# Moving a finished block's store and its subtractions behind the next statistics stores in GpSimd's queue

## The chip, the cores and the metric

The kernel runs on one core of one Trainium2 chip. The time is the device time of one execution in microseconds (us). Before the change it is 1297.03 us, the median of three runs that lie between 1296.88 and 1305.32 us.

Engines have short names in the profile: PE is TensorE (matrix products; PEld is its weight load), DVE is VectorE, ACT is ScalarE, POOL is GpSimd, and SP is SyncE, which here only issues transfers. A name with a q (SPq) is an engine's sequencer, which issues and waits. Each engine works through its own queue in order: an instruction that waits holds everything behind it on that engine.

## The reference

One layer with two branches over 1024 tokens of width 1024, in float32: a Mamba-2 scan and a causal attention with a forgetting term. Both are gated, projected, merged and projected again:

```python
h = _rmsnorm(x, pre_g)
proj = jnp.einsum('bld,de->ble', h, w_in)   # z_ssm, xbc, dt, q, k, v, f, z_att, g_ssm, g_att
# branch A: y_ssm = group-normed SSD scan, times silu(z_ssm)
# branch B, 16 heads of 64, blocks of 128 queries:
s = q @ k.T * scale + fcum[t] - fcum[s]      # causal
o = softmax(s) @ v
y_att = o * silu(z_att)
p_ssm = y_ssm @ w_branch_ssm
p_att = y_att @ w_branch_att
merged = sigmoid(g_ssm) * p_ssm + sigmoid(g_att) * p_att
out = x + _rmsnorm(merged @ w_out, post_g)
```

## The kernel before

**The projections.** All large products (the input projection, the two branch projections, the output projection) are made of 128x512 tiles with a seven-product scheme for 2x2 blocks (Winograd's form of Strassen's). For it, each right-hand operand is cut into four blocks `b11, b12, b21, b22`, and differences `t1 = b12 - b11`, `t2 = b22 - t1`, `t3 = t2 - b11`, `t4 = t2 - b21` are formed. Each operand is split into a high and a low part (`x0h`, `x0l` for b11, `x1` for b21, `x2` for -b22, `x3` for t1, `x4` for -t2, `x5` for t3, `x6` for t4) and multiplied three times. A `Stream` object doles these products out in halves, as work that fills TensorE while a latency-bound stage runs.

**The attention.** It runs over eight head pairs `hp` (two heads, 128 channels, 1024 tokens), from about 690 to 1150 us of the span. For seven pairs there are five visits each (`JOINED`, line 1384); the last pair has six (`SINGLE`). A visit makes scores `s` (TensorE), adds the forgetting term and takes a row minimum (VectorE, line 1558, tiles `ex`, `nm`), takes the exponential (ScalarE, line 1563), transposes the result (TensorE, `pt`), copies it out of PSUM (`p`, lines 1600 and 1602) and multiplies it with `v` into `av`. Between its parts, fixed numbers of stream halves are placed. A pair's output comes in three groups n = 0, 1, 2, which end with its visits g = 1, 3 and 4. Groups 0 and 1 make up the second half of the tokens (h = 1), group 2 is the first half (h = 0). For each group:

- `settle` and `scale` (lines 1436 to 1455) make the softmax denominators from small tiles: `nr`, `dd`, `sm`, `ns`, of 128x4 and 128x8 elements;
- `send` (line 1457) transposes `ns` (`tp`), copies the 8x128 result to `st` (ScalarE, line 1463) and stores it in DRAM with two transfers from GpSimd's queue (line 1465): a row of statistics;
- `take` (line 1467) loads it back, spread over 64 partitions each (`rb`, line 1471, SyncE's queue);
- `free` (line 1482) multiplies `av` by the gate `zr` into `o`, which frees the PSUM bank (line 1490);
- `out` (line 1492) multiplies `o` by `rb`: lines 1502 and 1503 for n = 0 and 1, line 1496 for n = 2. After n = 1 and n = 2 a half of the pair's output stands in the tile `zr`, which has two buffers, and `outputs` (line 1629) is called.

**A finished block.** For all pairs but the last, `outputs` stores the half to `ya_dram` (line 1633, GpSimd's queue) and makes the differences that the branch projection needs later, on GpSimd: for pairs 0 to 3 `t1` from h = 0 alone (line 1639, on a tile `y` that is loaded from `ya_dram`), for pairs 4 to 6 `t2` and `t3` after h = 1 (lines 1645 and 1646) and `t4` after h = 0 (line 1659), on a tile `x` of one buffer, which holds `t1`. Results are stored later as chores of the stream (line 196). GpSimd also makes the like differences of the other branch in this stage (line 214), sums of weights (line 364) and transfers to `ms_dram` (line 1104).

**What sets the order.** The main loop (line 1722) goes through the visits m. In each it makes scores, then calls `out` for the group that ended two visits ago, then `weighted`, then `free` and `send` for the group that ended one visit ago. So `out(1)` of a pair and `send(2)` of the same pair fall into one iteration, in that order; `out(2)` falls into the next one, where nothing is sent; `send(0)` of the next pair comes an iteration later. Operations in `pin(...)` keep their program order on their engine. The others (SyncE's loads among them, lines 266, 1477, 1679) are placed by a scheduler, by its own estimate of when they can run. `attended` records which halves are stored; a block of `ya_dram` is loaded as an operand only after that (lines 297 to 315).

## Time and profile before

| What | us |
| --- | --- |
| median of three runs | 1297.03 |
| the profiled execution, whole | 1297.4 |
| its span, first to last instruction | 1295.6 |
| PE busy | 1251.2 (97%) |
| DVE busy | 1018.6 (79%) |
| ACT busy | 796.9 (62%) |
| POOL busy | 288.6 (22%) |

The granted TensorE clock is 0.996 in the mean. All times in the text are us from the first instruction of this execution. In a row of the timeline stand the start, the time taken, the engine, the line, the operation and its tiles; in brackets stands how long the engine had been idle before it and what ended that. In rows of waits stand the engine that waited, what it waited for, the sum, the number of times and the longest.

### The profile page before, as it was taken

The page shows a single profiled execution, that of the slowest core. Times are in us where ns is not written, and L with a number is a line of the kernel's source. Part 1 is how long each engine was busy: PE and PEld are TensorE (multiplying, and loading weights), DVE is VectorE, ACT ScalarE, POOL GpSimd, SP SyncE. Part 2 cuts the span into 40 slices and gives each one's busy share as a digit, 9 for nine tenths or more (in the row PEclk, how much of TensorE's full clock was granted, in tenths as well). Part 3 has the DMA queues.
Part 4 walks back from the last instruction along what each step waited for, and adds up shares of the span by engine and source line. Part 5 has one row for each costly group of instructions (what it writes and reads, how often), then busy time and mean ns, then how long its engine had stood idle before and what let it go on. Part 6 is the DMA issues. An engine that isn't in the chain of part 4 may idle for free.

```text
span 1295.6 us, 21107 instructions
## 1 busy us (share of the span) xinstructions
PE 1251.2 (97%) x7066; PEld 987.7 (76%) x7066; DVE 1018.6 (79%) x1979; ACT 796.9 (62%) x1728; POOL 288.6 (22%) x307
## 2 busy tenths in 40 slices
PE   6999999999999999899999999999998999999998
PEld 4787888788887888688777777777777777678886
DVE  6998888798789878788677767676677877886976
ACT  8745666476556756566556566666667656753754
POOL 0000330024102320133001222222120313246052
PEclk9999999999999999999999999999999999999999
DMA  7332443654463544455474765666587657765932
GB/s 280 100 108 82 146 149 120 199 139 147 130 205 114 159 149 164 121 150 151 160 246 149 243 193 167 229 212 205 194 275 249 214 191 245 245 209 194 369 110 102
DMA packets 154669, 233.60 MB, mean 180 GB/s; under 512 B 17216, under 2 KB 62656, under 8 KB 154560
## 3 DMA queue, kind: packets, MB, share of 16 engines
q1 hardware_dynamic: 142016, 205.53, 49.5%
q0 software_dynamic: 6400, 16.10, 3.3%
q10 hardware_dynamic: 6144, 10.62, 2.2%
q8 instruction: 56, 0.92, 0.3%
q14 instruction: 53, 0.43, 0.1%
HBM read 162.99 MB, written 72.34 MB: 182 GB/s over the span
## 4 chain that ended last, share of the span: by engine, by line
PE 66%; DVE 10%; DMA 9%; issue 7%; ACT 6%; SPq 1%; POOL 1%; ACTq 0%; DVEq 0%; POOLq 0%
PE pb L130 28%; PE pc L130 16%; PE pd L130 5%; PE pt L133 4%; PE s L130 4%; PE av L130 4%; PE yps L130 2%; DVE wop L357 2%; DMA raw<-in_wu 1%; PE tr L133 1%; ACT ex L1563 1%; PE st L130 1%; ACT wop L355 1%; DMA rb<-st_dram 1%; DVE sum L364 1%
## 5 line engine op out<-in xcount | busy, mean ns | idle before, releaser
L357 DVE TENSOR_TENSOR wop<-sum,wop 128x512 fp32r<-128x512 f32 x174 | 137.8, 793 | 59.7 <-ACT wop L355 56.4
L355 ACT ACTIVATE wop<-sum 128x512 fp32r<-128x512 f32 x174 | 108.9, 627 | 99.5 <-DVE sum L364 48.3
L1563 ACT ACTIVATE ex<-ex,nm 128x512 f32<-128x512 f32 (+1 forms) x192 | 116.1, 606 | 58.5 <-DVE nm L1558 55.5
L412 ACT ACTIVATE s<-pb 128x512 f32<-128x512 f32 x141 | 83.7, 594 | 99.0 <-PE pb L130 82.3
L357 DVE TENSOR_TENSOR wop<-raw,wop 128x512 fp32r<-128x512 f32 x149 | 108.3, 729 | 42.6 <-ACT wop L355 42.3
L130 PE MATMUL pc<-x3h,wop 128*128 128x512 f32 x384 | 131.2, 398 | 3.4 <-ACT wop L355 2.0
L130 PE MATMUL pb<-x0h,wop 128*128 128x512 f32 x384 | 133.0, 402 | 0.7 <-ACT x0h L1253 0.6
L130 PE MATMUL pc<-x2h,wop 128*128 128x512 f32 x384 | 131.9, 400 | 0.0
L130 PE MATMUL pb<-x6h,wop 128*128 128x512 f32 x376 | 128.7, 398 | 1.2 <-ACT s L412 1.2
L130 PE MATMUL pb<-x5h,wop 128*128 128x512 f32 x376 | 127.9, 397 | 1.4 <-ACT s L412 1.3
L130 PE MATMUL pb<-x4h,wop 128*128 128x512 f32 x376 | 127.8, 397 | 0.2 <-DVE wop L357 0.2
L355 ACT ACTIVATE wop<-raw 128x512 fp32r<-128x512 f32 x151 | 94.1, 625 | 19.1 <-PE pc L130 9.2
L1558 DVE CUSTOM_DVE_ANT_0 ex<-s,fb 128x512 f32<-128x512 f32 (+1 forms) x192 | 96.4, 552 | 10.8 <-PE s L130 10.7
L130 PE MATMUL pd<-x1h,wop 128*128 128x512 f32 x264 | 89.1, 396 | 0.0
L130 PEld LDWEIGHTS pc<-x3h,wop 128*128 128x128 f32 x384 | 72.1, 188 | 21.5 <-issue 3.4
L130 PEld LDWEIGHTS pb<-x0h,wop 128*128 128x128 f32 x384 | 73.1, 190 | 17.4 <-ACT x0h L1253 1.3
L130 PEld LDWEIGHTS pc<-x2h,wop 128*128 128x128 f32 x384 | 72.1, 188 | 16.8 <-issue 1.5
L130 PEld LDWEIGHTS pb<-x5h,wop 128*128 128x128 f32 x376 | 70.6, 188 | 17.9 <-ACT s L412 2.7
L130 PEld LDWEIGHTS pb<-x6h,wop 128*128 128x128 f32 x376 | 70.9, 189 | 16.9 <-ACT s L412 1.6
L130 PEld LDWEIGHTS pb<-x4h,wop 128*128 128x128 f32 x376 | 70.4, 188 | 16.4 <-DVE wop L357 1.0
L214 POOL TENSOR_TENSOR wd<-wd 128x256 f32<-128x256 f32 x32 | 31.8, 995 | 226.9 <-DMA wd<-in_wo 107.7
L130 PE MATMUL s<-k,q 64*128 64x512 f32 (+3 forms) x576 | 72.8, 367 | 5.9 <-ACT p L1602 3.3
(341 smaller groups left out, 3015.1 us busy)
## 6 DMA issues: line engine op xcount, KB each, us to landing
raw<-in_wu SPq DMA_DIRECT2D x128, 256.0 KB, 3.8
csb<-cs_dram SPq DMA_DIRECT2D x32, 256.0 KB, 5.4
fb<-f_dram SPq DMA_DIRECT2D x16, 512.0 KB, 6.1
rb<-st_dram SPq DMA_DIRECT2D x48, 128.0 KB, 3.5
wd<-in_wo SPq DMA_DIRECT2D x40, 128.0 KB, 3.2
xt<-in_x SPq DMA_DIRECT2D x8, 512.0 KB, 5.8
gs_dram<-th ACTq DMA_DIRECT2D x16, 256.0 KB, 3.4
qh_dram<-th SPq DMA_DIRECT2D x16, 256.0 KB, 4.2
```

Source lines behind the costliest of these rows:

```text
L130: return tc.keep_in_program_order(nc.tensor.matmul(*args, **kw))
L133: return tc.keep_in_program_order(nc.tensor.transpose(out_, in_, idn))
L214: pin(nc.gpsimd.tensor_tensor(t[out_], t[a_], t[b_], ALU.subtract))
L355: nc.scalar.activation(op[:, 0], src, AF.Copy, scale=sign)
L357: nc.vector.tensor_tensor(op[:, 1], src, op[:, 0], ALU.subtract)
L364: self.adds.tensor_tensor(t, x, y, ALU.add)
L412: nc.scalar.activation(s, ps, AF.Copy)
L1558: nc.vector.tensor_tensor_reduce(to, bank(u, e), fb[hp, h][:, e, 0 : w[u]], 1.0, 3.0e38, ALU.add, ALU.min, nm)
L1563: nc.scalar.activation(to, to, AF.Exp, scale=-1.0, bias=nm, accum_out=hd.at(hd.sm, i, h, e))
```

## The change

`outputs` no longer issues the store and the subtractions of pairs 0 to 6. It puts them on a list, `behind_rows`, and the main loop issues them right after the next `send`. The arithmetic is the same. For pairs 0 to 3 the load of `y` stays where it was. The last pair's subtractions are on VectorE, as before.

```diff
         def outputs(hp, h, zr):
+            if hp < NK - 1:
+                y = fetched("b12", hp) if hp < KH and h == 0 else state.get("y")
+                behind_rows.append(lambda: differences(hp, h, zr, y, state.get("t")))
+                return
             attended.add((hp, h))
-            if hp < NK - 1:
-                pin(nc.gpsimd.dma_start(ya_dram[hp, :, half(h)], zr))
-
-            eng = nc.vector if hp == NK - 1 else nc.gpsimd
+            j, x, y = hp - KH, state["t"], state["y"]
+            pin(nc.vector.tensor_tensor(x, zr, x, ALU.subtract))
+            pin(nc.vector.tensor_tensor(y, x, y, ALU.subtract))
+            ops_a.put(j, t2=x, t3=y, b22=zr)
+
+        behind_rows = []
+
+        def differences(hp, h, zr, y, x):
+
+            attended.add((hp, h))
+            pin(nc.gpsimd.dma_start(ya_dram[hp, :, half(h)], zr))
             if hp < KH:
                 if h == 0:
-                    y = fetched("b12", hp)
                     pin(nc.gpsimd.tensor_tensor(y, y, zr, ALU.subtract))
                     stream.chores += [None, lambda: ops_a.store("t1", hp, y)]
                 return
...
                 hd.free(which)
                 if m < NV:
                     hd.send(which)
+                    while behind_rows:
+                        behind_rows.pop(0)()
             stream.release()
```

GpSimd's queue about the end of pair 0 and the beginning of pair 1, before. The first row stores the half h = 1, the second group 2's statistics, the fifth and sixth handle h = 0, and the last stores the statistics of pair 1's group 0; line 214 belongs to the other branch.

```order
L1633 DMA ya_dram<-zr 128x512
L1465 DMA st_dram<-st 2x2x128 x2
L214 TENSOR_TENSOR x<-x,th 128x512
L196 DMA t_s<-x 128x512
L1633 DMA ya_dram<-zr 128x512
L1639 TENSOR_TENSOR y<-y,zr 128x512
L214 TENSOR_TENSOR x<-x,th 128x512
L1465 DMA st_dram<-st 2x2x128 x2
```

The same place of the same queue now (line 1633 has become 1646, line 1639 has become 1649):

```order
L1465 DMA st_dram<-st 2x2x128 x2
L1646 DMA ya_dram<-zr 128x512
L214 TENSOR_TENSOR x<-x,th 128x512
L196 DMA t_s<-x 128x512
L214 TENSOR_TENSOR x<-x,th 128x512
L1465 DMA st_dram<-st 2x2x128 x2
L1646 DMA ya_dram<-zr 128x512
L1649 TENSOR_TENSOR y<-y,zr 128x512
```

Group 2's statistics no longer stand behind the store of h = 1, and the store and the subtraction of h = 0 have moved behind the statistics of the next pair.

GpSimd's queue at the end of pair 4, before, where h = 1 has two subtractions and h = 0 one:

```order
L1633 DMA ya_dram<-zr 128x512
L1645 TENSOR_TENSOR x<-zr,x 128x512
L1646 TENSOR_TENSOR y<-x,y 128x512
L1465 DMA st_dram<-st 2x2x128 x2
L196 DMA t_a<-x 128x512
L196 DMA t_a<-y 128x512
L1633 DMA ya_dram<-zr 128x512
L1659 TENSOR_TENSOR x<-x,zr 128x512
L196 DMA t_a<-x 128x512
L1465 DMA st_dram<-st 2x2x128 x2
```

And now (1645 has become 1654, 1646 has become 1655, 1659 has become 1664):

```order
L1465 DMA st_dram<-st 2x2x128 x2
L1646 DMA ya_dram<-zr 128x512
L1654 TENSOR_TENSOR x<-zr,x 128x512
L1655 TENSOR_TENSOR y<-x,y 128x512
L196 DMA t_a<-x 128x512
L196 DMA t_a<-y 128x512
L1465 DMA st_dram<-st 2x2x128 x2
L1646 DMA ya_dram<-zr 128x512
L1664 TENSOR_TENSOR x<-x,zr 128x512
L196 DMA t_a<-x 128x512
```

Both statistics stores now stand ahead of the work on the block beside them.

ScalarE's queue early in the last pair, as a piece of the difference. `x1h<-x1l` splits a b21 block that was loaded from `ya_dram`; `ex` is the exponential of the scores:

```order
 L412 ACTIVATE s<-pb 128x512
 L355 ACTIVATE wop<-raw 128x512
-L281 ACTIVATE x1h<-x1l 128x512 x2
-L1563 ACTIVATE ex,sm<-ex,nm 128x512 x4
+L281 ACTIVATE x1h<-x1l 128x512
+L1563 ACTIVATE ex,sm<-ex,nm 128x512
+L281 ACTIVATE x1h<-x1l 128x512
+L1563 ACTIVATE ex,sm<-ex,nm 128x512 x3
 L278 ACTIVATE x4h<-x4l 128x512
 L281 ACTIVATE x1h<-x1l 128x512
```

The second split, which is of the block of pair 6, h = 0, now stands between the first exponential of the visit and the other three. In SyncE's queue, the load of that block has moved from ahead of group 0's two `rb` loads to behind them. TensorE's queue holds the same instructions in the same order as before.

## The prediction

> **What bounds the kernel now.** I read the busy table first. These are its first two lines: the span, and each engine's busy time.

> ```profile
> span 1295.6 us, 21107 instructions
> PE 1251.2 (97%) x7066; PEld 987.7 (76%) x7066; DVE 1018.6 (79%) x1979; ACT 796.9 (62%) x1728; POOL 288.6 (22%) x307
> ```

> TensorE is the bound, and it has 1295.6 - 1251.2 = 44.4 us of idle time in all. Its queue is unchanged, so the change can only fill or widen these gaps. Where they lie is told by the busy time per stage; this is the attention from 700 to 1140 us (stage, its length, busy PE, PEld, DVE, ACT, POOL, clock, DMA share, GB/s):

> ```profile
> 700.00:1140.00 440.00, 424.68 (x2891) 324.68 (x2889) 325.02 (x813) 286.79 (x710) 100.28 (x134) 1.00 0.66 219
> ```

> 440.0 - 424.7 = 15.3 us. This is the ceiling of any gain here: 1.2% of the time. It is further out of reach since the waits of TensorE from 690 to 1150 us name neither GpSimd nor a transfer:

> ```profile
> PE pt L133 <- ACT ex L1563: 3.4, 3, 1.9
> PE s L130 <- ACT p L1602: 3.3, 2, 2.8
> PE s L130 <- DVE p L1600: 2.5, 4, 1.0
> ...
> PE pc L130 <- DVE th L422: 0.5, 1, 0.5
> ```

> So I looked for what stands behind the gaps. The timeline about the largest of them (2.77 us) shows it, engine by engine: TensorE, VectorE, ScalarE, GpSimd, at the end of pair 0.

> ```profile
> 744.51 1.98 PE L130 MATMUL s<-k,q 64*128 64x512 f32 x12 [2.77 <-ACT p L1602]
> ...
> 737.14 0.69 DVE L1496 TENSOR_TENSOR zr<-o,rb 128x512 f32<-128x512 f32 x1 [1.41 <-DMA rb<-st_dram]
> ...
> 738.35 2.92 DVE L1436 TENSOR_TENSOR nr<-nm 128x4 f32<-128x4 f32 x1
> ...
> 741.58 0.21 ACT L1439 ACTIVATE dd<-dd 128x8 f32<-128x8 f32 x1 [5.00 <-DVE dd L1438]
> ...
> 738.14 0.58 POOL L1633 DMA_DIRECT2D ya_dram<-zr  x1 [7.75 <-DVE zr L1496]
> 738.73 1.29 POOL L1639 TENSOR_TENSOR y<-y,zr 128x512 f32<-128x512 f32 x1
> 739.97 1.28 POOL L214 TENSOR_TENSOR x<-x,th 128x512 f32<-128x512 f32 x1
> ```

> The chain reads: VectorE sits 1.41 us for the statistics `rb`; then `nr`, four elements a partition, takes 2.92 us and ends as GpSimd's two subtractions end (739.97 + 1.28 = 741.25); ScalarE, whose `dd` comes next in its queue, is idle 5.00 us; the copies `p` behind it are late; TensorE waits 2.77 us. All executions of that line on VectorE, with least, median and longest time in ns:

> ```profile
> L1436 DVE TENSOR_TENSOR nr<-nm x15: 154/156/2924, 703.8 to 1113.5; 128x4 f32<-128x4 f32 x15
> ```

> The median is 0.156 us, so `nr` was held for 2.77 us. Two things on this chain are touched by the change: the wait for `rb`, and the subtraction of h = 0.

> **The change part by part.**

> *Statistics ahead of the store of h = 1 (seven pairs).* How often line 1496 waits for `rb` is in VectorE's waits of the stage:

> ```profile
> DVE zr L1496 <- DMA rb<-st_dram: 8.3, 6, 2.4
> ```

> The longest is pair 6, again by engines: ScalarE, GpSimd, VectorE, TensorE.

> ```profile
> 1081.54 0.25 ACT L1463 ACTIVATE st<-tp 8x128 f32<-8x128 f32 x1
> ...
> 1081.81 0.57 POOL L1633 DMA_DIRECT2D ya_dram<-zr  x1 [3.26 <-DVE zr L1503]
> 1082.39 1.30 POOL L1645 TENSOR_TENSOR x<-zr,x 128x512 f32<-128x512 f32 x1
> 1083.78 1.62 POOL L1646 TENSOR_TENSOR y<-x,y 128x512 f32<-128x512 f32 x1
> 1085.35 1.17 POOL L1465 DMA_DIRECT2D st_dram<-st  x2
> ...
> 1093.53 0.69 DVE L1496 TENSOR_TENSOR zr<-o,rb 128x512 f32<-128x512 f32 x1 [2.39 <-DMA rb<-st_dram]
> ...
> 1100.14 0.55 PE L130 MATMUL s<-k,q 64*128 64x128 f32 x6 [1.00 <-DVE p L1600]
> ```

> `st` is ready at 1081.79, yet its store goes out at 1085.35. Ahead of the block's work it can go some 3.3 us sooner, more than the 2.39 us of the wait. For pairs 0 to 3 only the store's issue (0.57 us) and the wait for the block stand ahead of it, so there it gains less than in pairs 4 to 6; I take the 8.3 us as gone. It is VectorE's time, not TensorE's: what it is worth is the gap that follows.

> *Subtractions of h = 0 out of the denominator chain (seven).* They now run some 13 us later (738.7 becomes 752.2 below). Besides pair 0, pair 3 shows the hold (`sm` on VectorE, then TensorE):

> ```profile
> 904.46 2.82 DVE L1450 TENSOR_TENSOR sm<-sm,dd 128x8 f32<-128x8 f32 x1 [0.28 <-ACT dd L1439]
> ...
> 909.15 1.66 PE L130 MATMUL s<-k,q 64*128 64x512 f32 x11 [0.70 <-DVE p L1600]
> ```

> TensorE's gaps within some 7 us behind a line 1496 that waited are then 2.77 (pair 0), 0.70 (pair 3), 1.00 (pair 6) and the 0.5 for `th`, line 422 (pair 4): 4.97 us at most. Of this I count 4 us, since line 214 stays and will still hold something, and the gaps of 1.00 and 0.5 have a nearer cause of their own.

> *Where they go.* Behind the statistics of the next pair, here pair 1 (GpSimd, then VectorE):

> ```profile
> 750.49 1.15 POOL L1465 DMA_DIRECT2D st_dram<-st  x2 [9.24 <-ACT st L1463]
> ...
> 752.52 0.69 DVE L357 TENSOR_TENSOR wop<-raw,wop 128x512 fp32r<-128x512 f32 x1 [2.91 <-ACT wop L355]
> ```

> The subtraction would run from 750.49 + 1.15 + 0.58 = 752.2 to 753.5 and hold `wop` of line 357 for about 1 us. `wop` is prepared three steps of the stream ahead, and VectorE has been idle 2.91 us before it. Such holds exist now: 45 of these have a mean of 802 ns against 686 for the like `wop<-sum`,

> ```profile
> L357 DVE TENSOR_TENSOR wop<-raw,wop 128x512 fp32r<-128x512 f32 x45 | 36.1, 802 | 32.9 <-ACT wop L355 32.8
> L357 DVE TENSOR_TENSOR wop<-sum,wop 128x512 fp32r<-128x512 f32 x35 | 24.0, 686 | 10.7 <-ACT wop L355 8.0 <-PE s L130 2.7
> ```

> so 45 x 0.116 = 5.2 us are lost there already, while TensorE's waits above name no `wop`. I put this at 0; if the cover is gone, it is 7 x 1.29 = 9.0 us at the very most. The store of h = 0 moves with it: `zr` has two buffers, and its reload moves behind `rb` in SyncE's queue. I price that at 0, bounded by the next part.

> *The last pair.* This part costs. The block of pair 6, h = 0, is stored later, and its split has landed between two exponentials. Rows of GpSimd, SyncE, ScalarE, TensorE:

> ```profile
> 1104.29 1.17 POOL L1465 DMA_DIRECT2D st_dram<-st  x2 [3.39 <-ACT st L1463]
> ...
> 1104.11 1.33 SPq L266 DMA_DIRECT2D x1l<-ya_dram  x3
> 1108.76 1.09 SPq L1471 DMA_DIRECT2D rb<-st_dram  x2
> ...
> 1108.76 1.14 ACT L281 ACTIVATE x1h<-x1l 128x512 fp32r<-128x512 f32 x2
> 1110.64 0.73 ACT L1563 ACTIVATE ex<-ex,nm 128x512 f32<-128x512 f32 x1
> ...
> 1113.18 0.71 ACT L1563 ACTIVATE ex<-ex,nm 128x512 f32<-128x512 f32 x1
> ...
> 1114.25 1.91 PE L133 MATMUL pt<-ident,ex 128*128 128x128 f32 x16
> ```

> The store goes out at 1104.29 + 1.17 = 1105.46. From issue to landing it takes 2.6 us, the load 3.5 us (medians), and a store of the tile `zr` 5.2 us at the longest:

> ```profile
> ya_dram<-zr POOLq DMA_DIRECT2D x14, 256.0 KB, 2.6
> x1l<-ya_dram SPq DMA_DIRECT2D x3, 256.0 KB, 3.5
> ...
> DMA to landing us min/median/max: 2.3/2.7/5.2
> ```

> It lands at 1108.1; SyncE first issues `rb` until 1109.85, so the load goes at 1109.9 and lands at 1113.4. Split and three exponentials, 0.57 + 3 x 0.72 = 2.7, end at 1116.1. The transposes that stand at 1114.25 need them: TensorE loses 1.9 us. With 5.2 for both transfers it is 1105.46 + 5.2 + 5.2 + 2.7 - 1114.25 = 4.3 us; at the least nothing, if the load is as quick as it need be.

> *The sum* against the profiled execution: 1297.4 - 4.0 + 1.9 = 1295.3. It lies 0.4 above the median of the runs shown, so the median comes to 1294.9, or 1295.

> **The rivals.**

> *The holds move and cost the same.* For it: GpSimd's 1.29 us are spent wherever they stand, and two subtractions still stand side by side in some rows. Against it: the other holds of `wop` have no gap behind them. Then the collisions give nothing and the waits for `rb` at most the 1.00 and 0.5: 1297.0 - 1.5 + 1.9 = 1297.4, no change.

> [...]

> *The last pair's split decides (slower).* The exponentials wait on a transfer that passes GpSimd's and SyncE's queues, and the holds move too: 1297.0 + 1.9 to 4.3 = 1299 to 1301. It decides if the store takes over 5 us, as the longest does, or if SyncE is held at the load. To go beyond 1% it would need 13 us, three times the worst sum; something that I have not seen would have to join it, a late `zr` reload above all.

> *All gaps of the stage close.* 15.3 us, 1281.7: the gaps that stand nowhere near a line 1496 (`tp` and most of `pt`) would have to go with them. Little speaks for it.

> **How the numbers follow.** A run of this kernel can be told from no change by about 1%, 13 us. The forecast, a gain of 0.5 to 5 us (1292 to 1296.5), gets 0.53; no change, 1296.5 to 1298, 0.22; the slower rival within 1% 0.20; slower by over 1% 0.03; faster by over 1% 0.02. Hence same 0.95. For the range: the whole gain with no loss in the last pair is 1297.0 - 5.0 = 1292.0, and I leave 1 us more for the 0.4 by which the profiled execution and the median differ, so 1291; above, the middle of the slower rival, 1300.

> **What would show it.** In the changed profile, line 1496 should wait for `rb` for under 2 us in all; lines 1436 and 1450 should have no execution near 2.8 us; the gap ahead of `s` at 744 should be under 1 us. The first exponentials of the last pair should show an idle ScalarE of some 3 us with the load of `x1l` named, and a TensorE gap of about 2 us ahead of `pt` there. The forecast is wrong if new gaps stand about 2 us behind the `st` stores of group 0, where the subtractions have gone, or if `zr` loads hold line 1490.

## The result, and the profile after

The changed kernel takes 1288.76 us (median of 6 runs, 1285.58 to 1289.88) where the kernel before takes 1298.75 beside it (6 runs, 1296.88 to 1305.32). The ratio is 0.9913, 95% interval 0.9888 to 0.9937. The forecast was 1295, range 1291 to 1300, with 95% on "within 1%": the direction is right and the gain is about five times too small. The profiled execution of the changed kernel took 1288.93 us. Its span and busy times:

```profile
span 1287.2 us, 21110 instructions
PE 1247.7 (97%) x7066; PEld 986.4 (77%) x7066; DVE 1018.2 (79%) x1979; ACT 796.8 (62%) x1728; POOL 285.8 (22%) x307
```

The span is 8.4 us shorter, and these two lines split it in two parts. TensorE's idle time went from 44.4 to 1287.2 - 1247.7 = 39.5 us, 4.9 less. TensorE's busy time also fell, from 1251.2 to 1247.7, 3.5 less, for the same 7066 matmuls. The trace of before has one stretch at half clock more than that of the changed kernel (3.41 us from 978.55 us, shown below); it accounts for an estimated 1.7 of the 3.5 (half of 3.41), and the rest is spread in small steps whose cause is open. The prediction had a term for the first part alone.

The attention stage, in the columns shown for before (stage, length, busy PE, PEld, DVE, ACT, POOL, clock, DMA share, GB/s):

```profile
700.00:1140.00 440.00, 428.56 (x2911) 328.21 (x2906) 329.59 (x820) 289.34 (x715) 101.46 (x135) 1.00 0.65 220
```

Idle TensorE there is 11.4 us instead of 15.3. TensorE's waits from 690 to 1150 us (us in all, times, longest):

```profile
PE tp L133 <- DVE nm L1558: 4.7, 6, 1.7
PE pb L130 <- ACT s L412: 1.9, 2, 1.2
PE pt L133 <- ACT ex L1563: 1.6, 2, 1.2
PE s L130 <- ACT p L1602: 1.0, 1, 1.0
```

Ahead of `s`, the wait for ScalarE's `p` went from 3.3 us, longest 2.8, to one of 1.0. Ahead of `pt`, the longest fell from 1.9 to 1.2. Next, the two lines of the denominators on VectorE, with least, median and longest time in ns:

```profile
L1436 DVE TENSOR_TENSOR nr<-nm x15: 152/156/165, 703.1 to 1106.4; 128x4 f32<-128x4 f32 x15
...
L1450 DVE TENSOR_TENSOR sm<-sm,dd x15: 158/166/169, 704.4 to 1110.8; 128x8 f32<-128x8 f32 x15
```

The holds of 2.9 and 2.8 us are gone from both. VectorE's wait for the statistics, from 700 to 1140 us:

```profile
DVE zr L1496 <- DMA rb<-st_dram: 7.9, 3, 3.8
```

In sum it hardly fell (8.3 before), against the forecast of under 2. It left the pairs 0, 4 and 5. Pair 6 kept 2.23 us of 2.39, and in pair 3 it grew from 1.73 us to 3.79. The third of the three is that of the last pair, 1.90 us; before, it stood at 1146 us with 1.65, outside the stretch, so that the pairs 0 to 6 go from 8.3 to 6.0. Pair 3, by rows of VectorE, GpSimd, SyncE and TensorE:

```profile
901.60 0.69 DVE L1496 TENSOR_TENSOR zr<-o,rb 128x512 f32<-128x512 f32 x1 [3.79 <-DMA rb<-st_dram]
...
894.12 1.30 POOL L214 TENSOR_TENSOR x<-x,th 128x512 f32<-128x512 f32 x1 [3.33 <-DMA th<-ys_dram]
...
895.45 1.72 SPq L1471 DMA_DIRECT2D rb<-st_dram  x2
...
905.46 1.71 PE L130 MATMUL s<-k,q 64*128 64x512 f32 x11 [1.05 <-ACT p L1602]
```

The load of `rb` goes out 0.03 us after line 214 ends (894.12 + 1.30). `rb` and line 214's `th` come from the same ring of small tiles, so the order of queues left one wait on a reader of that ring. TensorE waits 1.05 us behind it, where it waited 0.70 before.

GpSimd's holds did not shrink either. They moved onto `wop`, here in pair 2 (VectorE, then GpSimd):

```profile
802.93 3.24 DVE L357 TENSOR_TENSOR wop<-raw,wop 128x512 fp32r<-128x512 f32 x1
...
803.08 1.30 POOL L1649 TENSOR_TENSOR y<-y,zr 128x512 f32<-128x512 f32 x1
804.33 1.29 POOL L214 TENSOR_TENSOR x<-x,th 128x512 f32<-128x512 f32 x1
```

Here `wop` takes 3.24 us instead of 0.69, and no gap of TensorE over 0.3 us stands between 777.8 and 904.4 us.

### The profile page after: what moved, and what is told of

The parts are those of the page before. It is cut to its first block, busy times and chain, and to the rows that moved or that the text cites. A ratio compares the mean times of both kernels' runs of the same rounds, so it can differ in the third digit from the quotient of the medians.

```text
span 1287.2 us, 21110 instructions
## 1 busy us (share of the span) xinstructions
PE 1247.7 (97%) x7066; PEld 986.4 (77%) x7066; DVE 1018.2 (79%) x1979; ACT 796.8 (62%) x1728; POOL 285.8 (22%) x307
## 4 chain that ended last, share of the span: by engine, by line
PE 62%; DVE 12%; DMA 9%; issue 7%; ACT 6%; SPq 2%; POOL 1%; ACTq 0%; DVEq 0%; POOLq 0%
PE pb L130 27%; PE pc L130 15%; PE pd L130 5%; PE pt L133 3%; PE av L130 3%; PE s L130 3%; DVE wop L357 3%; PE yps L130 2%; PE tr L133 1%; DVE ex L1558 1%; PE st L130 1%; ACT ex L1563 1%; ACT wop L355 1%; DMA xt<-in_x 1%; DVE sum L364 1%
## 5 line engine op out<-in xcount | busy, mean ns | idle before, releaser
L357 DVE TENSOR_TENSOR wop<-sum,wop 128x512 fp32r<-128x512 f32 x174 | 137.0, 789 | 59.5 <-ACT wop L355 59.1
L355 ACT ACTIVATE wop<-sum 128x512 fp32r<-128x512 f32 x174 | 108.8, 626 | 99.3 <-DVE sum L364 45.3
L1563 ACT ACTIVATE ex<-ex,nm 128x512 f32<-128x512 f32 (+1 forms) x192 | 116.0, 605 | 55.2 <-DVE nm L1558 54.8
L357 DVE TENSOR_TENSOR wop<-raw,wop 128x512 fp32r<-128x512 f32 x149 | 114.5, 770 | 35.6 <-ACT wop L355 35.4
L130 PE MATMUL pc<-x3h,wop 128*128 128x512 f32 x384 | 131.2, 398 | 3.1 <-ACT wop L355 1.7
L130 PE MATMUL pb<-x0h,wop 128*128 128x512 f32 x384 | 132.6, 401 | 0.7 <-ACT x0h L1253 0.5
L130 PE MATMUL pc<-x2h,wop 128*128 128x512 f32 x384 | 131.8, 400 | 0.0
L130 PE MATMUL pb<-x5h,wop 128*128 128x512 f32 x376 | 128.0, 397 | 1.9 <-ACT s L412 1.9
L130 PE MATMUL pb<-x6h,wop 128*128 128x512 f32 x376 | 128.3, 397 | 1.1 <-ACT s L412 1.1
L130 PE MATMUL pb<-x4h,wop 128*128 128x512 f32 x376 | 127.6, 397 | 0.3 <-DVE wop L357 0.3
L1558 DVE CUSTOM_DVE_ANT_0 ex<-s,fb 128x512 f32<-128x512 f32 (+1 forms) x192 | 96.4, 552 | 12.2 <-PE s L130 12.1
L355 ACT ACTIVATE wop<-raw 128x512 fp32r<-128x512 f32 x151 | 94.0, 624 | 19.2 <-PE pc L130 11.2
L130 PE MATMUL pd<-x1h,wop 128*128 128x512 f32 x264 | 89.1, 396 | 0.0
L130 PEld LDWEIGHTS pc<-x3h,wop 128*128 128x128 f32 x384 | 72.1, 188 | 21.1 <-ACT wop L355 3.4
L130 PEld LDWEIGHTS pb<-x0h,wop 128*128 128x128 f32 x384 | 72.9, 190 | 17.4 <-ACT x0h L1253 1.5
L130 PEld LDWEIGHTS pc<-x2h,wop 128*128 128x128 f32 x384 | 72.1, 188 | 16.5 <-issue 1.5
L130 PEld LDWEIGHTS pb<-x5h,wop 128*128 128x128 f32 x376 | 70.6, 188 | 18.2 <-ACT s L412 3.0
L130 PEld LDWEIGHTS pb<-x6h,wop 128*128 128x128 f32 x376 | 70.6, 188 | 16.6 <-ACT s L412 1.5
L130 PEld LDWEIGHTS pb<-x4h,wop 128*128 128x128 f32 x376 | 70.5, 188 | 16.0 <-issue 0.7
L214 POOL TENSOR_TENSOR wd<-wd 128x256 f32<-128x256 f32 x32 | 31.7, 990 | 225.9 <-DMA wd<-in_wo 124.7
L130 PE MATMUL pb<-x0l,wop 128*128 128x512 f32 x192 | 75.7, 394 | 0.7 <-DVE x0l L1255 0.7
## 6 DMA issues: line engine op xcount, KB each, us to landing
raw<-in_wu SPq DMA_DIRECT2D x128, 256.0 KB, 3.7
csb<-cs_dram SPq DMA_DIRECT2D x32, 256.0 KB, 5.0
gs_dram<-th ACTq DMA_DIRECT2D x16, 256.0 KB, 3.5
qh_dram<-th SPq DMA_DIRECT2D x16, 256.0 KB, 5.0
```

Of the source, the lines that this page charges most:

```text
L130: return tc.keep_in_program_order(nc.tensor.matmul(*args, **kw))
L214: pin(nc.gpsimd.tensor_tensor(t[out_], t[a_], t[b_], ALU.subtract))
L355: nc.scalar.activation(op[:, 0], src, AF.Copy, scale=sign)
L357: nc.vector.tensor_tensor(op[:, 1], src, op[:, 0], ALU.subtract)
L1558: nc.vector.tensor_tensor_reduce(to, bank(u, e), fb[hp, h][:, e, 0 : w[u]], 1.0, 3.0e38, ALU.add, ALU.min, nm)
L1563: nc.scalar.activation(to, to, AF.Exp, scale=-1.0, bias=nm, accum_out=hd.at(hd.sm, i, h, e))
```

## The experiments

Three theories stood against each other. **Statistics**: the gain is the wait of line 1496 for `rb`. **Hold**: it is GpSimd's subtraction, which held the denominators. **Chain**: both stand one behind the other on VectorE with some slack behind them, so that a gap of TensorE is wait + hold - slack. The first results brought a fourth question, the **clock**.

All runs in one table. "Clock" is the mean granted clock of the runs, and "lost" the mean of (1 - clock) x span, the time that the lowered clock takes. The last column is the mean time less that; it is an estimate, since it takes all the lowered clock as lost time. A run's clock is listed to 0.001, which is 1.3 us.

| kernel | runs | median us | ratio to before, 95% interval | clock | lost us | mean less lost |
|---|---|---|---|---|---|---|
| before, beside the experiments | 60 | 1298.1 | | 0.9948 | 6.8 | 1291.4 |
| changed, both sets of runs | 12 | 1288.9 | 0.9913 (0.9888 to 0.9937); 0.9935 (0.9916 to 0.9954) | 0.9977 | 3.0 | 1285.9 |
| h = 1 alone | 6 | 1290.92 | 0.9940 (0.9921 to 0.9959) | 0.9960 | 5.2 | 1285.8 |
| h = 0 alone | 12 | 1292.72 | 0.9959 (0.9944 to 0.9973) | 0.9973 | 3.4 | 1289.5 |
| before, no subtractions | 7 | 1289.05 | 0.9941 (0.9919 to 0.9962) | 0.9963 | 4.8 | 1285.8 |
| changed, no subtractions | 6 | 1289.79 | 0.9940 (0.9918 to 0.9961) | 0.9960 | 5.2 | 1284.7 |
| pair 6 put back | 6 | 1287.97 | 0.9928 (0.9908 to 0.9948) | 0.9970 | 3.9 | 1284.5 |
| store of h = 0 at once | 8 | 1291.66 | 0.9953 (0.9935 to 0.9972) | 0.9966 | 4.4 | 1287.4 |
| five long stretches | 4 | 1322.71 | 1.0197 (1.0169 to 1.0226) | 0.9860 | 18.5 | 1304.8 |
| fifteen shorter stretches | 4 | 1342.89 | 1.0357 (1.0325 to 1.0389) | 0.9865 | 18.1 | 1325.4 |
| four stretches of 3.0 us | 4 | 1311.77 | 1.0105 (1.0084 to 1.0126) | 0.9908 | 12.1 | 1299.4 |
| fifteen of 0.8 us | 4 | 1306.62 | 1.0067 (1.0051 to 1.0084) | 0.9978 | 2.9 | 1303.6 |

**The parts, each alone.** The block of h = 1 alone behind the statistics:

```diff
             if hp < NK - 1:
                 y = fetched("b12", hp) if hp < KH and h == 0 else state.get("y")
+                if h == 0:
+                    differences(hp, h, zr, y, state.get("t"))
+                    return
                 behind_rows.append(...)
```

> Only the block of h = 1 goes behind the statistics; the block of h = 0 is stored and subtracted at once, as before. Beside it the kernel before measures 1298.75 us and the changed one 1288.76. If the gain is the wait for rb alone (the statistics theory), this kernel has all of it: 1289 to 1291. If it is the hold of VectorE by the subtraction of h = 0 alone (the hold theory), it has almost nothing: 1297 to 1299. If wait and hold lie in one chain with a slack, so that a gap is wait + hold - slack (the chain theory, which I hold), each part alone closes some of each gap: here 1.41 (pair 0) + 1.51 (pair 4) + 0.70 (pair 3) + 1.00 (pair 6) = 4.6 us, 1294.

The block of h = 0 alone: the same edit with `if h == 1`.

> Only the block of h = 0 goes behind the next statistics; that of h = 1 stands ahead of them, as before. Statistics theory: no gain and the cost of the last pair, 1299 to 1300. Hold theory: all the gain, 1288 to 1290. Chain theory: the holds of pair 0 (2.77), pair 4 (1.19), pair 3 (0.70) and pair 1 (0.58) go, 5.2 us, less 1.2 us in the last pair: 1294 to 1295. If the two parts add up plainly, the gains of this kernel and of the one with h = 1 alone make 10 us together; if either closes the same gap, they make more.

Measured beside 1298.48 for before: 1290.92 and 1292.72, gains of 7.6 and 5.8 us. The first lies in the range that the statistics theory gave it (1289 to 1291), but by that theory the second would have no gain at all; the hold theory misses both. So neither theory of a single cause stands: each part alone has over half of the gain. Together they would make 13.4, the whole change makes 9 to 10: in part they close the same gaps, as the chain theory says. Its sizes (4.6 and 4 us) are too small for both, and its sum for h = 0 counted 0.58 us behind pair 1 as a hold, where the rows of before show none: VectorE waits there for a store of `gs_dram` (2.76 us).

Behind pair 0 the chain can be read row by row. First the kernel with h = 1 alone (VectorE, then TensorE):

```profile
735.83 1.55 DVE L1438 TENSOR_TENSOR dd<-nr,nm 128x4 f32<-128x4 f32 x2
...
737.86 1.27 DVE L1451 TENSOR_TENSOR sm<-sm 128x4 f32<-128x4 f32 x1
...
741.46 1.29 PE L130 MATMUL s<-k,q 64*128 64x512 f32 x7 [0.92 <-ACT p L1602]
```

and the one with h = 0 alone:

```profile
738.51 0.69 DVE L1496 TENSOR_TENSOR zr<-o,rb 128x512 f32<-128x512 f32 x1 [1.91 <-DMA rb<-st_dram]
...
740.42 1.29 DVE L1450 TENSOR_TENSOR sm<-sm,dd 128x8 f32<-128x8 f32 x1 [0.28 <-ACT dd L1439]
...
744.23 1.69 PE L130 MATMUL s<-k,q 64*128 64x512 f32 x7 [1.62 <-ACT p L1602]
```

In the first there is no wait for `rb`, and two holds, of `dd` (1.32 us over its usual 0.23) and of `sm` (1.11). In the second there is a wait of 1.91, and line 214 alone holds `sm` (1.12). Wait, hold and gap of each kernel at this place, in us:

| kernel | wait for `rb` | hold | wait + hold - 1.41 | gap of TensorE |
|---|---|---|---|---|
| before | 1.41 | 2.77 | 2.77 | 2.77 |
| before, second profile | 1.78 | 2.77 | 3.14 | 3.13 |
| h = 1 alone | 0 | 2.44 | 1.03 | 0.92 |
| h = 0 alone | 1.91 | 1.12 | 1.62 | 1.62 |
| before, no subtractions | 1.80 | 0.94 | 1.33 | 1.33 |
| changed | 0 | 1.09 | 0 | none |

The slack of 1.41 is set by the first row, and the other five follow from it within 0.11. That the hold of before equals its gap was an accident: wait and slack happened to be the same. The slack belongs to this place. In pair 3 it is another, and not even one number: with a wait and no hold, as in the changed kernel, the gap is the wait less 2.74 to 2.76 us (four profiles); where a hold comes in, as in both profiles of before, the slack is 3.69.

**The holds priced by leaving them out.** In the kernel before, without GpSimd's subtractions:

```diff
-                    pin(nc.gpsimd.tensor_tensor(y, y, zr, ALU.subtract))
...
-                pin(eng.tensor_tensor(x, x, zr, ALU.subtract))
```

and the two of h = 1 for the last pair only.

> The kernel before without GpSimd's four subtraction lines for the pairs 0 to 6 (y - zr, x - zr, zr - x, x - y are left out, so the second multiplication gets other operands; every store and load stays). It prices the hold itself. Hold theory: the gain of the change or more, 1287 to 1290. Chain theory: 2.77 + 1.19 + 0.70 + 0.58 = 5.2 us and no loss in the last pair, 1293 to 1294. Statistics theory: within 1 us of before, 1298.

It measured 1289.05, in the range of the hold theory and about as fast as the changed kernel, with waits for `rb` left in it. So taking the hold away is worth about what the change is worth, and so is the order of the statistics (h = 1 alone): less the clock's part, both come to 1285.8. The chain theory's 1293 is too slow here too.

The same lines left out of the changed kernel:

> The changed kernel without GpSimd's subtractions for the pairs 0 to 6 (left out as in the kernel before without them; every store and load stays; the orders of the other engines are those of the changed kernel). It prices the holds at their new place. If they cost nothing there: as the changed kernel, 1288 to 1289.5. If the holds of line 357 (24.9 us of held VectorE in the trace) still reach TensorE: 1284 to 1286.

It measured 1289.79 beside 1297.62, no better than the changed kernel. At their new place, in front of `wop`, the holds cost the time nothing that these runs can show. One thing may hide a gain: in this kernel's profile, of its slowest run (1293.20), ScalarE idles 5.95 us in the last pair for the load of `x1l`, TensorE waits 3.06 us behind it, and 6.83 us at half clock follow. The changed kernel has 2.86 and 0.38 us there.

**The clock.** The kernel before, unchanged, as a control:

> The kernel before, unchanged, as a control of spread and clock. In its profile the granted clock fell to a half for 3.4 us at about 978 us, and the changed kernel's profile has no such stretch there: clock 0.996 against 0.998. If that stretch belongs to the kernel before, all its runs show 0.996; if it comes by chance, some show 0.998 and are about 1.7 us shorter. Time 1297 to 1300, ratio 1.000 within 0.002.

It measured 1298.57, ratio 1.0003 (0.9987 to 1.002), with clocks from 0.991 to 0.996 over its 12 runs: the stretch at half clock belongs neither to each run nor to one place. Its profile shows such a stretch behind pair 0 too, where the first profile has none. First the windows of the control (window, length, busy PE and the other engines, clock):

```profile
740.59:744.00 3.41, 1.10 (x7) 0.79 (x9) 2.58 (x6) 2.49 (x6) 0.00 (x0) 1.00 0.75 261
744.00:747.41 3.41, 3.41 (x17) 1.90 (x17) 3.22 (x9) 2.79 (x7) 0.00 (x0) 0.50 0.20 73
```

then those of the first profile of before, at the same place in the program and in pair 4:

```profile
739.57:742.98 3.41, 2.18 (x14) 1.59 (x12) 3.07 (x8) 0.88 (x3) 1.68 (x2) 1.00 0.45 156
742.98:746.39 3.41, 1.88 (x12) 1.19 (x12) 2.50 (x6) 3.01 (x7) 0.00 (x0) 1.00 0.54 193
746.39:749.80 3.41, 3.41 (x24) 2.30 (x24) 3.13 (x8) 2.78 (x8) 0.00 (x0) 1.00 0.25 77
...
975.14:978.55 3.41, 1.14 (x7) 0.62 (x6) 2.50 (x4) 3.41 (x9) 1.10 (x2) 1.00 0.51 191
978.55:981.96 3.41, 3.41 (x16) 3.22 (x15) 2.40 (x4) 3.41 (x8) 0.00 (x0) 0.50 0.42 92
```

The stretches last 3.41 us (3413 ns in the clock records of the trace) and begin at whole multiples of 3.413 us from each other: in the first profile at 545.06 and 978.55, which is 433.49 = 127.0 x 3.413. Laid out in such windows, a window with 2.3 us of idle TensorE is followed by one at half clock, in which TensorE loses an estimated 1.7 us (half of 3.41). The gap of 2.77 us in the first profile fell across the edge at 742.98, 1.23 us on one side and 1.53 on the other, and nothing followed. So the theory: what counts is the idle time within one window, and where a gap falls in the windows is chance.

The test puts idle time into the changed kernel, once in a few long pieces and once in many short ones. PAIRS, GROUPS and COUNT stand for what sets the two apart: in the second form pairs 1 to 4, group 0 and 8 for the long ones, pairs 1 to 5, all three groups and 2 for the short ones; in the first form the long ones had five pairs too.

```diff
                 tp = pp.tile([P, HALF], F32, tag="s", bufs=4, name="tp")
                 turn(tp[0:8, 0:P], self.ns[n].rearrange("p h e t -> p (h e t)"))
-                st = small("st")[0:8, 0:P]
+                whole = small("st")
+                st = whole[0:8, 0:P]
+                if self.hp in PAIRS and n in GROUPS:
+                    dum = whole[:, 256:512]
+                    pin(nc.gpsimd.memset(dum, 0.0))
+                    turn(tp[0:8, P : 2 * P], dum[:, 0:8])
+                    for _ in range(COUNT):
+                        pin(nc.gpsimd.memset(dum, 0.0))
+                    turn(tp[0:8, P : 2 * P], dum[:, 0:8])
```

In a first form these lines stood behind the copy of `st`.

> The changed kernel with five idle stretches of TensorE put in, one behind the transposition of the statistics of group 0 in the pairs 1 to 5: TensorE waits for eight small memsets of GpSimd, about 8 x 0.3 + 0.3 = 2.7 us each, 13.5 us in all. Theory of the clock: a 3.41 us window of TensorE with more than about 1.6 us idle is followed by 3.41 us at half clock (1.7 us lost), so nearly each of the five long stretches costs 1.7 us more than itself: clock 0.991 to 0.993, time about 1288.8 + 13.5 + 7.5 = 1310. If the stretches at half clock come by chance, the clock stays at 0.998 and the time is that of the kernel with the short stretches, 1302.

> As the kernel with five long stretches, but fifteen short ones of TensorE, behind the statistics of all three groups in the pairs 1 to 5, two memsets each: 2 x 0.3 + 0.3 = 0.9 us, 13.5 us in all as well. Theory of the clock: none of them reaches 1.6 us, so the clock stays as in the changed kernel, 0.997 to 0.999, and the time is 1288.8 + 13.5 = 1302 or less (other waits shrink). If any idle time lowers the clock, it falls as with the long ones.

This form missed its aim: the first added transposition waited 1.7 us in the mean, at most 2.4, for the copy of `st`, so the short stretches were 1.7 + 0.8 us and the long ones 1.7 + 3.0. The 0.3 us a memset in what was expected is an estimate; what was measured is 3.0 us for a wait behind eight and 0.8 behind two. Both lowered the clock to 0.986, and told nothing apart. In the second form the lines stand ahead of the copy, as above.

> The changed kernel with four idle stretches of TensorE put in, behind the transposition of the statistics of group 0 in the pairs 1 to 4: TensorE waits there for eight memsets of GpSimd, 3.0 us each as measured with the kernel of the five long stretches, 12 us in all; nothing else is waited for now. Theory of the clock: a window of 3.41 us with over 1.75 us idle is followed by 3.41 us at half clock, 1.7 us lost; a stretch of 3.0 us leaves such a window nearly always, so 4 x 1.7 = 6.8 us on top: 1288.8 + 12 + 6.8 = 1307 to 1308, clock lower by 0.005 than with the short ones. If the half clock comes by chance: 1301, clock as with the short ones.

> Fifteen idle stretches of 0.8 us (two memsets), behind the statistics of all three groups in the pairs 1 to 5, 12 us in all as with the four of 3.0 us. Theory of the clock: 0.8 us alone lowers no clock, so 1288.8 + 12 = 1301 and the clock of the changed kernel, 0.997 to 0.998. If all idle time of TensorE lowers the clock alike, the clock and the time are those of the four long stretches.

The clock of each profile, and what TensorE waited for, four long stretches first:

```profile
core 0: 1308.1 us, clock 0.992
```

```profile
PE tp L133 <- POOL st L1468: 12.0, 4, 3.0
```

and fifteen short ones:

```profile
core 0: 1306.4 us, clock 0.998
```

```profile
PE tp L133 <- POOL st L1468: 11.9, 15, 0.8
```

The idle time put in is the same, 12.0 and 11.9 us. The clock of the runs is 0.9908 against 0.9978: 12.1 us lost against 2.9, the latter what the changed kernel loses without any. Both medians lie 4 to 6 us above what was expected, and where that comes from is not shown; the clocks, and which of the two is slower, came as expected. In the profile of the long ones, half clock follows directly on two of the four stretches; the other two fell across an edge, with 1.90 us at the most in one window. The medians differ by 5.2 us, and by the last column the short ones have the longer time apart from the clock, partly for one other gap of 2.9 us that stands in their profile at 1001 us. So the clock falls by how the idle time is bundled, and it is shown that 12 us in long gaps cost more than 12 us in short ones.

From the TensorE rows of all fourteen profiles I worked out the idle time of every window that was itself at full clock, on the grid of each profile's stretches, the last 50 us of each left out:

| idle TensorE in a window of 3.41 us | windows | followed by half clock |
|---|---|---|
| under 1.4 us | 4938 | 0 |
| 1.4 to 1.9 us | 37 | 8 |
| over 1.9 us | 30 | 30 |

Of the 30, 14 lie between 532 and 544 us, ahead of the attention, where every kernel has such gaps; 3 more are in kernels without added idle time, and 13 in those with it.

**The last pair, and a faster kernel.** The changed kernel again, and two forms that give the last pair its early load back:

> The changed kernel once more, as the control of spread and clock on this chip: 1288.8 within 1, clock 0.997 to 0.999 in most runs, where the kernel before shows 0.992 to 0.997 beside it. If the clock belongs to the chip and not to the kernel, both show the same clock here.

> The changed kernel, but the block of h = 0 of pair 6 is stored and subtracted at once, so that the splits of the last pair stand where they stood before. If the last pair lost what the gaps there show (0.59 and 0.38 us, and 1.2 us of lag), this is the fastest: 1287 to 1288. If these gaps were already paid elsewhere: 1288 to 1290, no difference. Clock 0.998.

> The changed kernel, but the block of h = 0 is stored at once and only its subtraction goes behind the next statistics. The splits of the last pair then stand as in the kernel before, and line 1496 and the denominators keep what the change gave. If the last pair's later load cost 1 to 2 us: 1287 to 1288, as with pair 6 alone put back (1288.0). If the store itself ahead of the denominators did harm: 1289 to 1292.

```diff
+                if h == 0 and hp == NK - 2:
+                    differences(hp, h, zr, y, state.get("t"))
+                    return
                 behind_rows.append(...)
```

is the edit of the former; the latter issues the store of every h = 0 in `outputs` and leaves only the subtraction in `differences`. The control measured 1289.96, with a clock of 0.997 where before had 0.995 beside it, so the clock belongs to the kernel and not to the chip. Pair 6 put back measured 1287.97; its interval and that of the changed kernel overlap widely. The store at once measured 1291.66 beside the control's 1289.96, and these overlap too. What the last pair costs is below what can be told here, and no form beats the changed kernel by more than the spread.

## Why the prediction was right or wrong

**Right: the bound and the mechanism.** Most of TensorE's gaps behind line 1496 closed: 2.77 us behind pair 0 and 0.5 for `th` in pair 4 are gone, and the one of 1.00 behind pair 6 fell to 0.15. Pair 3 is the exception: its hold is gone, but its wait grew, and its gap went from 0.70 to 1.05. By rows and by the runs with one part alone, the mechanism is shown for pair 0. No gap appeared behind the statistics of group 0, and `wop` covers the holds there, as priced at 0. The rival by which the holds move and cost the same is refuted by the time, and the kernel without subtractions speaks against it, though its first half is true: they did move.

**Wrong, the step that failed: the sum.** It took only gaps "within some 7 us behind a line 1496 that waited", and it priced each at its own length. The ceiling of 15.3 us rests on the same step, since it takes TensorE's busy time as fixed.

The first half missed a gap some fifteen us further on, in pair 4. The rows of before, in order of time:

```profile
960.97 0.69 DVE L1496 TENSOR_TENSOR zr<-o,rb 128x512 f32<-128x512 f32 x1 [1.51 <-DMA rb<-st_dram]
...
962.48 1.35 DVE L1451 TENSOR_TENSOR sm<-sm 128x4 f32<-128x4 f32 x1
...
964.63 0.69 DVE L357 TENSOR_TENSOR wop<-raw,wop 128x512 fp32r<-128x512 f32 x1
...
965.35 0.33 SPq L348 DMA_DIRECT2D raw<-in_wbs  x1
...
966.35 1.93 SPq L266 DMA_DIRECT2D x5l<-t_s  x4
...
969.98 0.62 ACT L655 ACTIVATE th<-th 128x512 f32<-128x512 f32 x1
...
972.75 0.33 ACTq L656 DMA_DIRECT2D ga_dram<-th  x1
973.12 0.72 ACT L1563 ACTIVATE ex<-ex,nm 128x512 f32<-128x512 f32 x1 [2.53 <-DMA x5l<-t_s]
...
977.64 0.33 PE L133 MATMUL pt<-ident,ex 128*128 128x128 f32 x1 [1.89 <-ACT ex L1563]
```

ScalarE's store `ga_dram` is ready at 970.60 and is issued at 972.75; the profile names a load of `x5l` as what ended it. The exponentials behind it are late by as much, and TensorE waits 1.89 us. In the changed kernel:

```profile
953.95 0.69 DVE L1496 TENSOR_TENSOR zr<-o,rb 128x512 f32<-128x512 f32 x1
...
964.39 0.61 ACT L655 ACTIVATE th<-th 128x512 f32<-128x512 f32 x1
965.39 0.33 ACTq L656 DMA_DIRECT2D ga_dram<-th  x1
965.76 0.72 ACT L1563 ACTIVATE ex<-ex,nm 128x512 f32<-128x512 f32 x1 [0.76 <-DVE nm L1558]
...
970.39 1.80 PE L133 MATMUL pt<-ident,ex 128*128 128x128 f32 x12
```

There is no wait, no hold, and the store goes 0.4 us after its operand; the gap is gone. It is tempting to read one chain out of this: wait and hold make `wop` late, its end at 965.32 frees the `raw` that SyncE's next load waits for (965.35), and the loads of `x5l` behind it go late. But the kernel before without subtractions has neither a wait nor a hold in pair 4, and it has the gap all the same (VectorE, ScalarE, TensorE):

```profile
954.20 0.69 DVE L1496 TENSOR_TENSOR zr<-o,rb 128x512 f32<-128x512 f32 x1
...
963.40 0.61 ACT L655 ACTIVATE th<-th 128x512 f32<-128x512 f32 x1
...
966.17 0.33 ACTq L656 DMA_DIRECT2D ga_dram<-th  x1
...
971.07 0.33 PE L133 MATMUL pt<-ident,ex 128*128 128x128 f32 x1 [1.28 <-ACT ex L1563]
```

What goes with the gap stands in the instruction records of the traces, which name for each transfer the semaphore (a counter) that it raises when it has landed. In the kernel before, the store `ga_dram` raises the same one as the third of the four loads of `x5l`, and ScalarE's queue waits on it ahead of the store, until 972.70. In the changed kernel the store shares with the first load, which lands earlier:

| kernel (times in us) | wait, hold in pair 4 | store shares with | store held | gap ahead of `pt` |
|---|---|---|---|---|
| before | 1.51, 1.19 | third load | 2.15 | 1.89 |
| before, second profile | 0.10, 1.20 | third load | 2.25 | 1.38 |
| before, no subtractions | 0, 0 | third load | 2.16 | 1.28 |
| h = 1 alone | 0, 1.19 | third load | 1.09 | 0.20 |
| h = 0 alone | 1.06, 0 | first load | 0.29 | none |
| changed | 0, 0 | first load | 0.39 | none |

The other eight profiles share with the first load and have no gap ahead of `pt` there. So wait and hold can have made at most a part of the 1.89 us: without either, 1.28 are left. In every kernel in which work on pair 4's block of h = 0 was moved, the store has the other partner. No run changed the partner alone, and why the move changes it is not shown; as far as is known, this part of the gain is luck. The prediction had quoted this 1.9 and put it with the gaps that stand nowhere near a line 1496.

With this gap, and one of 0.58 in pair 1 that the second profile of before does not have, the gaps that closed make about 7 us, not 4. Pair 3's larger one, one of 1.18 ahead of `pb` in pair 5 and those of the last pair take part of it back, and 4.9 us are left on the page.

The second half is the clock, which the prediction had no term for. The two longest gaps of the attention before, 2.77 and 1.89 us, can put over 1.4 us of idle time into one window, and by the table above such a window is followed by half clock sometimes (8 times of 37) or, over 1.9 us, always (30 of 30). Behind 700 us, apart from the span's last stretch, the changed kernel's first profile has no stretch at half clock and its second has one; the first of before has one, its second three. Over all runs the mean time fell from 1298.2 to 1288.9, 9.3 us. Of that the clock is an estimated 6.8 - 3.0 = 3.8 us and the rest 5.5. The forecast was 2.1 for the rest (4.0 - 1.9), and 0 for the clock.

**Wrong in size: the waits for `rb`.** All 8.3 us were to go. In pair 6 the store does go out at once (1074.3 us, `st` being ready at 1074.0), yet only 0.2 us of the wait went: the second load of `rb` takes 5.4 us from issue to landing instead of some 3.2. Why it takes longer is open. In pair 3 the load itself went late, as shown above. The sum survived it because the gap counted for pair 6 shrank all the same.

**Wrong in size: the last pair.** The mechanism is there (ScalarE, then TensorE):

```profile
1105.08 0.63 ACT L281 ACTIVATE x1h<-x1l 128x512 fp32r<-128x512 f32 x1 [2.86 <-DMA x1l<-ya_dram]
...
1107.88 1.64 PE L133 MATMUL pt<-ident,ex 128*128 128x128 f32 x13 [0.38 <-ACT ex L1563]
```

ScalarE idles 2.86 us for the load, as forecast (some 3). TensorE idles 0.38 us there instead of 1.9, and 0.59 us ahead of `s` before that, a gap that before does not have. In sum this part cost about half of what was priced: the transposition `tp` of the pair's group 0 comes 8.68 us earlier than before (1093.95 against 1102.63), that of group 1 only 7.70 us (1114.43 against 1122.13), so 1.0 us against 1.9. The rival in which this decides had 0.20 and did not come in the changed kernel; its wait shows in one profile, that of the changed kernel without subtractions (3.06 us, above).

## What to carry to other kernels

Where a wait and a hold stand one behind the other, a gap of the bounding engine can be their sum less a slack (behind pair 0 of before 1.41 + 2.77 - 1.41 = 2.77 us). Take all three from the trace, and a part of a change can be priced at that place before it is tried; at another place the slack is another. Do not stop at a fixed time behind a cause, but test a path that two traces suggest on a third, of a kernel in which the supposed cause is absent: here the gap in pair 4 stayed. When an issue stands with its operand ready, look for which semaphore it waits: the two transfers that shared one here tied their queues together, and the store stood 2.15 us. Where TensorE is the bound, ask of each gap whether its idle time fills more than half of a clock window (1.9 of 3.41 us here): 12 us in four long gaps went with a clock of 0.9908 and 1311.77 us, 12 us in fifteen short ones with 0.9978 and 1306.62, so breaking up a long gap can pay even where its length stays.
